# Squares of the first input held as whole tiles and summed by two engines in turn, and a pooling state stored in long rows

## The chip, the cores and the metric

The kernel runs on one core of one Trainium2 chip. The metric is the time of one execution on the device in microseconds (us), as the median over several runs. A core has five engines that run their own queues of instructions in order and wait for one another by semaphores: PE (TensorE, matmuls; PEld is its loading of weights), DVE (VectorE), ACT (ScalarE), POOL (GpSimd) and SP (SyncE, which here issues DMAs). DMAs are issued from the queues of SP, ACT and POOL; "SPq" and "ACTq" in a row mean the issuing instruction in that queue.

## The reference

One step of a decoder of two layers, for a prompt of 1024 positions and for 8 sample rows of one position each. All is float32; D is 1024.

```
layer 0: h = rmsnorm(x); z = h @ w_in_ab          # columns: pooling mixer | RWKV-7
         mix = concat(pool_mix(z[:512]), rwkv7_mix(z[512:])) @ w_out_ab
layer 1: h = rmsnorm(x); mix = sgu_mix(h)          # gated MLP with position mixing
each:    x += mix; x += cross_attn(rmsnorm(x)); x += relu(rmsnorm(x) @ w_up)**2 @ w_down
last:    y = rmsnorm(x)
rmsnorm(x) = x * rsqrt(mean(x*x) + eps) * g
pool_mix: new state of a sample row = its last 15 rows of (old state of 15 rows, new row)
```

The outputs are y, the keys and values of the memory tokens, and the new states, among them the pooling state of the 8 sample rows (8 x 15 x 512 numbers), which the kernel stores as a tensor `ps` of 128 partitions x 480.

## The kernel before

Activations lie transposed: a tile is 128 channels by 1032 columns (1024 prompt positions and the 8 sample rows), and eight such tiles make up x. Matmuls are exact to float32 by splitting each operand into a high and a low part and adding three products (high-high, high-low, low-high); `split` makes the parts, the high one on ACT (L194 without, L197 with a scale) and the low one on DVE (L195, L198). Columns are worked on in three groups GR of 384, 384 and 264. Large tiles come from 42 slots that `get` and `put` hand out first in, first out; `m2` hands out pieces of 512 columns from a ring of four buffers. The tile framework fills each engine's queue, as a rule in the order in which the code is written, sometimes with an instruction put ahead, and adds the waits.

The first place of the change is the very start. `xs` below is new; before, the loop at L544 loads a tile of x (L547), splits it (L197 on ACT, L198 on DVE), and calls `Stats.add` for each of the three column groups. `Stats.add` squares on ACT (L261 for the first tile, L264 for the others, into an `m2` buffer) and adds the square to the accumulator on GpSimd (L265). The matmuls of the loop (L565) need only the split parts: two blocks of output columns (units 16 and 17 of w_in_ab) are accumulated over all eight tiles in six PSUM banks, 18 matmuls for a tile. After the loop `finish` sums the accumulator over the partitions by small matmuls (L271), scales on DVE (L273) and takes the power -1/2 on GpSimd (L274), and `spread` writes it along the columns (L287 on PE, L289 on ACT) as the row by which every output is multiplied (L607 on DVE). Only then are the six PSUM banks emptied, so the next block's matmuls (`linear_g`, L225 to L227) wait for all of this. That block's weights were loaded and are cast on ACT (L194) when the buffer that block 16 used is free, and their low part is made on GpSimd (L195 in POOL's queue, since WZ[0] is 1), ahead of L274 in its queue.

The second place lies 375 us later, where the recurrent part has begun. Its chain of small matmuls (`Chain`, L1175 to L1217) goes on beside three other streams: the pooling mixer (`pooling`, L931), the inverses of small triangular blocks on DVE (`inverses`, L907 and L908, then ACT L911 and the stores L912 and L913 to `xid`), and the keys of the memory tokens (`memkv`, L1028 to L1033: a block of weights loaded by SP L204, split, 24 matmuls, scaled by L1032, stored by L1033). At the end of `pooling` SP stores the new states: L969 the prompt's, L970 the samples'. The samples' state lies in `pb4`, 32 runs of 16 numbers on each partition, of which L970 stores the last 15 of each run, in a DMA of 4096 pieces of 15 numbers. Behind it in SP's queue stand the last store of the pooling mixer (L967), a store of keys (L1033), the next load of weights (L204), and the stores of the inverses. ACT's queue issues the loads of the recurrent part (L1124 to L1137), among them L1131.

A DMA counts on one of eight semaphores, taken in turn over all DMAs of SP and ACT, and waits until the DMA eight before it has landed; these waits stand in the rows of the queues as waits for a semaphore.

Of the kernel before, what the change touches and what calls it, by code (L numbers as in the profile page):

```python
# [13 lines left out]
AF = mybir.ActivationFunctionType  # L14
ALU = mybir.AluOpType
# [9 lines left out]
GR = ((0, 384), (384, 768), (768, 1032))  # L25
# [100 lines left out]
def hybrid_step(ctx: ExitStack, tc: tile.TileContext, I, O):  # L126
    nc = tc.nc
    te, ve, se, po, sy = nc.tensor, nc.vector, nc.scalar, nc.gpsimd, nc.sync
# [5 lines left out]
    def nm(s="t"):  # L134
        uid[0] += 1
        return f"{s}{uid[0]}"
# [5 lines left out]
    def get(dt=F32):  # L142
        i = free.popleft()
        t = sb.tile([128, T], dt, tag=f"s{i}", name=nm("s"))
        owner[id(t)] = (i, t)
        return t

    def put(*ts):
        for t in ts:
            free.append(owner.pop(id(t))[0])  # L150

    def small(shape, tag, bufs=2, dt=F32):
        return sb.tile(shape, dt, tag=tag, bufs=bufs, name=nm(tag))
# [10 lines left out]
    def cyc(key, tags):  # L164
        turn[key] = turn.get(key, -1) + 1
        t = tags[turn[key] % len(tags)]
        return ps_of(t, 2 if t == "lin" else 1)
# [6 lines left out]
    def psm():  # L174
        return cyc("m", ("in0", "in1", "c0b", "c1b") if wide[0] else ("in0", "in1"))
# [11 lines left out]
    def pc(name, i):  # L187
        c = PCOL[name] + i
        return par[:, c : c + 1]


    def split(src, hi, lo, scale=None, eng=None):
        if scale is None:
            se.copy(out=hi, in_=src)  # L194
            (eng or ve).tensor_tensor(out=lo, in0=src, in1=f(hi), op=ALU.subtract)  # L195
        else:
            se.activation(out=hi, in_=src, func=AF.Copy, scale=scale)  # L197
            ve.scalar_tensor_tensor(out=lo, in0=src, scalar=scale, in1=f(hi), op0=ALU.mult, op1=ALU.subtract)  # L198
# [93 lines left out]
    def hpair():  # L292
        return get(F32R), get(F32R)
# [233 lines left out]
    st0 = Stats()  # L527
    first, fraw = [], []

    def fload(j, c0, c1_):  # L530
        if j == len(first):
            raw = sb.tile([128, 1024], F32, tag="wraw", bufs=2, name=nm("wr"))
            hi, lo = [sb.tile([128, 1024], F32R, tag=t, bufs=2, name=nm(t)) for t in ("whi", "wlo")]
            fraw.append(raw)
            first.append((16 + j, (hi, lo)))
        raw, (hi, lo) = fraw[j], first[j][1]
        sy.dma_start(out=raw[:, c0:c1_], in_=wab[16 + j][:, c0:c1_])
        split(raw[:, c0:c1_], hi[:, c0:c1_], lo[:, c0:c1_])
# [2 lines left out]
    sy.dma_start(out=par, in_=I["par"])  # L541
    psf = {}
    h = []
    for m in range(KT):  # L544
        x, hp = get(), hpair()
        for g0, g1 in GR if m == 0 else ((0, T),):
            sy.dma_start(out=x[:, g0:g1], in_=I["xT"][m][:, g0:g1])  # L547
            split(x[:, g0:g1], hp[0][:, g0:g1], hp[1][:, g0:g1], pc("mix0", m))
        for g0, g1 in GR:
            st0.add(m, g0, g1, x[:, g0:g1])  # L550
        h.append(hp)
        put(x)
        if m == 0:
            fload(1, 0, 256)
        if m == 1:
            fload(0, 256, 1024)
            fload(1, 256, 1024)
            sy.dma_start(out=ident, in_=I["ident"])
        ks = slice(m * 128, (m + 1) * 128)
        for j, (u, (wh, wl)) in enumerate(first):  # L560
            for g, (g0, g1) in enumerate(GR):
                if m == 0:
                    psf[u, g] = cyc("f", ("lin", "lin", "c0a", "c1a", "c0b", "c1b"))[:, : g1 - g0]
                for i, (w, a) in enumerate(((wh, hp[0]), (wh, hp[1]), (wl, hp[0]))):
                    te.matmul(psf[u, g], w[:, ks], a[:, g0:g1], start=m == 0 and i == 0, stop=m == KT - 1 and i == 2)  # L565
    for g in range(3):
        st0.finish(g)
    tick()
# [84 lines left out]
    def bulk(n=1):  # L653
        for _ in range(n):
            next(zs_, None)
            if side and next(side[0], 0) == 0:
                side.popleft()
# [268 lines left out]
    pb4 = pbuf[:, 0:512].rearrange("p (g b t) -> p g b t", g=4, b=8)  # L926
    pin = pbuf[:, 512:992]
# [3 lines left out]
    def pooling():  # L931
        for g in range(4):
            zused[0] = zorder.index(g)
            while g not in zready:
                bulk()
                yield
            zused[0] += 1
            z = zready.pop(g)
            win = WIN[g]
            po.tensor_copy(out=ppo[:, g, :], in_=z[:, NP - 15 : NP])  # L940
            po.tensor_copy(out=pb4[:, g, :, 15:16].rearrange("p b t -> p (b t)"), in_=z[:, NP:T])
            cur, step = z, 1
            while step < win:
                nx = get()
                eng = (po, ve)[PG[{1: 0, 2: 4, 4: 8, 8: 12}[step] + g]]
                eng.tensor_tensor(out=nx[:, step:NP], in0=cur[:, step:NP], in1=cur[:, 0 : NP - step], op=ALU.add)
                po.tensor_copy(out=nx[:, 0:step], in_=cur[:, 0:step])
                if cur is not z:
                    put(cur)
                cur, step = nx, step * 2  # L950
            d = get()
            o = C1["cnt"][0] + 16 * g
            ve.scalar_tensor_tensor(out=d[:, 16:NP], in0=cur[:, 16:NP], scalar=1.0 / win, in1=z[:, 16:NP], op0=ALU.mult, op1=ALU.subtract)
            ve.tensor_tensor(out=cur[:, 0:16], in0=cur[:, 0:16], in1=c1[:, o : o + 16], op=ALU.mult)
            ve.tensor_tensor(out=d[:, 0:16], in0=cur[:, 0:16], in1=z[:, 0:16], op=ALU.subtract)
            t = small([128, 8], "pws")
            ve.tensor_reduce(out=t, in_=pb4[:, g, :, 16 - win : 16], axis=AX.X, op=ALU.add)
            ve.scalar_tensor_tensor(out=d[:, NP:T], in0=t, scalar=1.0 / win, in1=z[:, NP:T], op0=ALU.mult, op1=ALU.subtract)
            put(cur)
            bulk()  # L960
            for _ in range(PLY):
                yield
            for g0, g1 in GR:
                ps = psm()
                te.matmul(ps[:, : g1 - g0], g2t[:, 512 + g * 128 : 640 + g * 128], d[:, g0:g1], start=True, stop=True)
                se.activation(out=z[:, g0:g1], in_=ps[:, : g1 - g0], func=AF.Copy, scale=pc("psc", g))
            sy.dma_start(out=mixd[g], in_=z)  # L967
            put(z, d)
        sy.dma_start(out=O["pp"], in_=ppo)  # L969
        sy.dma_start(out=O["ps"].rearrange("p (n t) -> p n t", t=15), in_=pb4[:, :, :, 1:16].rearrange("p g b t -> p (g b) t"))  # L970
        put(pbuf, g2t, c1)
        yield

# [289 lines left out]

    segs = [[(0, n)] * (n < 4) + [(1, n - 1)] * (n > 0) for n in range(5)]
    pg = pooling()

    def start(n):
# [897 lines left out]
```

## Time and profile before

| what | before |
|---|---|
| median of 3 runs | 3179.05 us |
| lowest and highest run | 3176.22 and 3179.43 us |
| the profiled execution's own time | 3185.59 us |
| its span, first to last instruction | 3183.8 us |
| mean granted TensorE clock | 0.983 |
| busy: PE, DVE, ACT, POOL | 97%, 66%, 43%, 23% of the span |

The profile is one execution seen by the hardware profiler. A row of a timeline begins with its start in us from the start of the span and its length in us, then the engine, the line of the code, the operation, and the tiles (buffer numbers left out); "x3" means three such instructions merged into one row, with the length from the first to the end of the last. Brackets at the end give the idle time of the engine before the row and what ended it. A row of the windows view gives the start and end of a stretch, and for each engine its busy time and number of instructions, then the TensorE clock that was granted (1.00 is full), the mean share of time in which the 16 DMA engines were busy (overlapping transfers count twice), and what they moved in GB/s. A row of the grouped lines ends in its total, the mean in ns of one, and the idle time before.

### The profile page before, as it was taken

The numbers are of one execution on the slowest core, as the hardware profiler recorded it, in microseconds if no ns is written. First come the engines' busy times: TensorE is split into PE (matmuls) and PEld (weight loads), VectorE is DVE, ScalarE is ACT, GpSimd is POOL, SyncE is SP. The second block draws the span as 40 slices with busy tenths as digits, with TensorE's granted clock in tenths as the row PEclk, the third lists the DMA queues.
The fourth block names the chain that finished last, engine by engine and source line by source line (L and its number), as shares of the span: only waits on it lengthen the run. The fifth ranks groups of instructions, "written<-read, shape, count | busy, mean of one in ns | idle before, by whom it ended". The sixth has DMA issues, their size and how long they took to land. (4 is left out here: it accounts for less than half of the span.)

```text
span 3183.8 us, 59345 instructions
## 1 busy us (share of the span) xinstructions
PE 3081.0 (97%) x23514; PEld 2957.1 (93%) x23514; DVE 2086.6 (66%) x3778; ACT 1353.3 (43%) x2757; POOL 717.3 (23%) x650
## 2 busy tenths in 40 slices
PE   8999889999999999999999999999999999999998
PEld 7987778899899999999999999899989999999998
DVE  4688734644457887566787776656455788765775
ACT  5223234433345444544455454614334544453443
POOL 5233424320021223022131100223001122211213
PEclk9999989999999999999999999999999999999999
DMA  3346577643522444866522223524343244476643
GB/s 119 117 132 208 88 247 234 209 140 120 180 87 103 158 160 173 218 174 174 174 89 99 88 94 138 204 80 143 113 147 120 94 158 156 164 236 140 181 166 121
DMA packets 215846, 473.25 MB, mean 149 GB/s; under 512 B 47374, under 2 KB 72334, under 8 KB 215567
## 3 DMA queue, kind: packets, MB, share of 16 engines
q1 hardware_dynamic: 188814, 423.63, 39.0%
q0 software_dynamic: 6912, 25.37, 4.6%
q10 hardware_dynamic: 19840, 20.45, 2.3%
q8 instruction: 185, 3.03, 0.4%
q14 instruction: 95, 0.77, 0.1%
HBM read 309.87 MB, written 159.50 MB: 147 GB/s over the span
## 5 line engine op out<-in xcount | busy, mean ns | idle before, releaser
L454 PE MATMUL ps<-s,wp 128*128 128x258 f32 x3584 | 1018.7, 284 | 11.3 <-DVE s L490 5.9
L456 PE MATMUL ps<-s,wp 128*128 128x258 f32 x3584 | 1013.2, 283 | 4.4 <-DVE wp L195 4.2
L455 PE MATMUL ps<-s,wp 128*128 128x258 f32 x3584 | 1014.1, 283 | 0.0
L454 PEld LDWEIGHTS ps<-s,wp 128*128 128x128 f32 x3584 | 677.8, 189 | 15.2 <-DVE s L490 6.7
L456 PEld LDWEIGHTS ps<-s,wp 128*128 128x128 f32 x3584 | 678.9, 190 | 5.7 <-DVE wp L195 5.7
L455 PEld LDWEIGHTS ps<-s,wp 128*128 128x128 f32 x3584 | 680.5, 190 | 0.2 <-issue 0.2
L225 PE MATMUL ps<-s,wh 128*128 128x384 f32 (+2 forms) x1994 | 649.5, 327 | 19.3 <-ACT wh L194 16.5
L226 PE MATMUL ps<-s,wh 128*128 128x384 f32 (+2 forms) x1994 | 643.6, 323 | 0.1
L227 PE MATMUL ps<-s,wl 128*128 128x384 f32 (+2 forms) x1994 | 640.0, 322 | 0.4 <-DVE wl L195 0.4
L225 PEld LDWEIGHTS ps<-s,wh 128*128 128x128 f32 x1994 | 380.6, 191 | 30.4 <-ACT wh L194 17.3
L226 PEld LDWEIGHTS ps<-s,wh 128*128 128x128 f32 x1994 | 381.1, 191 | 7.9 <-issue 6.0
L227 PEld LDWEIGHTS ps<-s,wl 128*128 128x128 f32 x1994 | 380.0, 191 | 6.0 <-issue 4.1
L265 POOL TENSOR_TENSOR s<-s,m 128x384 f32<-128x384 f32 (+1 forms) x147 | 162.0, 1110 | 652.6 <-ACT m L264 651.7
L194 ACT CAST s<-s 128x516 fp32r<-128x516 f32 (+6 forms) x316 | 199.2, 657 | 144.2 <-DMA s<-hts 32.5
L195 DVE TENSOR_TENSOR wp<-wr,wp 128x512 fp32r<-128x512 f32 x200 | 159.9, 800 | 89.9 <-ACT wp L194 88.1
L194 ACT CAST wh<-wr 128x1024 fp32r<-128x1024 f32 x110 | 115.1, 1047 | 200.1 <-PE ps L226 155.1
L194 ACT CAST wp<-wr 128x512 fp32r<-128x512 f32 x200 | 124.5, 622 | 129.1 <-issue 48.3
L195 DVE TENSOR_TENSOR wl<-wr,wh 128x1024 fp32r<-128x1024 f32 x97 | 121.5, 1254 | 58.5 <-ACT wh L194 53.9
L195 DVE TENSOR_TENSOR s<-s,s 128x516 fp32r<-128x516 f32 (+6 forms) x148 | 122.5, 841 | 52.2 <-ACT s L194 40.5
L225 PE MATMUL ps<-s,s 128*128 128x384 f32 (+3 forms) x432 | 142.9, 333 | 6.9 <-ACT s L1768 6.5
L195 DVE TENSOR_TENSOR s<-s 128x516 fp32r<-128x516 f32 x168 | 116.3, 726 | 37.5 <-ACT s L194 37.0
L226 PE MATMUL ps<-s,s 128*128 128x384 f32 (+3 forms) x432 | 139.6, 323 | 0.0
(346 smaller groups left out, 5271.3 us busy)
## 6 DMA issues: line engine op xcount, KB each, us to landing
hdn<-s SPq DMA_DIRECT2D x128, 258.0 KB, 2.1
hts<-s SPq DMA_DIRECT2D x48, 516.0 KB, 2.7
s<-hts SPq DMA_DIRECT2D x96, 258.0 KB, 6.6
xf<-s POOLq DMA_DIRECT2D x48, 516.0 KB, 7.5
s<-hdn SPq DMA_DIRECT2D x72, 258.0 KB, 5.4
s<-in_wd SPq DMA_DIRECT2D x34, 512.0 KB, 5.2
s<-in_kc SPq DMA_DIRECT2D x64, 256.0 KB, 3.6
s<-in_vc SPq DMA_DIRECT2D x64, 256.0 KB, 3.1
```

The source lines that it names most:

```text
L194: se.copy(out=hi, in_=src)
L195: (eng or ve).tensor_tensor(out=lo, in0=src, in1=f(hi), op=ALU.subtract)
L225: te.matmul(out, wh, xh, start=i == 0, stop=False)
L226: te.matmul(out, wh, xl, start=False, stop=False)
L227: te.matmul(out, wl, xh, start=False, stop=i == n - 1)
L265: po.tensor_tensor(out=self.acc[:, g0:g1], in0=self.acc[:, g0:g1], in1=sq, op=ALU.add)
L454: te.matmul(out, wh, xh, start=j < 4 and k == 0, stop=False, skip_group_check=j >= 4)
L455: te.matmul(out, wh, xl, start=False, stop=False, skip_group_check=j >= 4)
L456: te.matmul(out, wl, xh, start=False, stop=k == 3, skip_group_check=j >= 4)
```

## The change

At the first place the squares are no longer taken group by group. A tile's square is taken by one ACT instruction over all 1032 columns into a slot of its own (the first tile's straight into the accumulator), and it is added by one instruction: on GpSimd for odd tiles, on DVE for even ones. This is done when two more tiles of x have been split; the last two squares follow after the loop. At the second place GpSimd first copies the 32 x 15 numbers of each partition into `pin` (the loaded old state, no longer needed), and the DMA stores `pin`, 480 numbers in a row on each partition.

```
+    def squares(m, x):
+        if m == 0:
+            se.activation(out=st0.acc, in_=x, func=AF.Square)
+        else:
+            sq = get()
+            se.activation(out=sq, in_=x, func=AF.Square)
+            (po if m % 2 else ve).tensor_tensor(out=st0.acc, in0=st0.acc, in1=sq, op=ALU.add)
+            put(sq)
+        put(x)
+    xs = deque()
     for m in range(KT):
...
-        for g0, g1 in GR:
-            st0.add(m, g0, g1, x[:, g0:g1])
+        xs.append((m, x))
         h.append(hp)
-        put(x)
+        if len(xs) > 2:
+            squares(*xs.popleft())
...
+    while xs:
+        squares(*xs.popleft())
     for g in range(3):
         st0.finish(g)
...
-        sy.dma_start(out=O["ps"].rearrange("p (n t) -> p n t", t=15), in_=pb4[:, :, :, 1:16].rearrange("p g b t -> p (g b) t"))
+        po.tensor_copy(out=pin.rearrange("p (n t) -> p n t", t=15), in_=pb4[:, :, :, 1:16].rearrange("p g b t -> p (g b) t"))
+        sy.dma_start(out=O["ps"], in_=pin)
```

How the queues change. First DVE's queue at the start, from the low part of the third tile to the first scaling in `finish`; `s_69` is the accumulator, each other `s` a slot, and par the table of scales. Before:

```order
L198 SCALAR_TENSOR_TENSOR s_166<-s_164,par,s_165 128x1032
L198 SCALAR_TENSOR_TENSOR s_199<-s_197,par,s_198 128x1032
L198 SCALAR_TENSOR_TENSOR s_232<-s_230,par,s_231 128x1032
L198 SCALAR_TENSOR_TENSOR s_265<-s_263,par,s_264 128x1032
L198 SCALAR_TENSOR_TENSOR s_298<-s_296,par,s_297 128x1032
L198 SCALAR_TENSOR_TENSOR s_331<-s_329,par,s_330 128x1032
L273 TENSOR_SCALAR rst_366<-ps_362 128x3
```

And now:

```order
L198 SCALAR_TENSOR_TENSOR s_154<-s_152,par,s_153 128x1032
L552 TENSOR_TENSOR s_69<-s_69,s_210 128x1032
L198 SCALAR_TENSOR_TENSOR s_179<-s_177,par,s_178 128x1032
L198 SCALAR_TENSOR_TENSOR s_206<-s_204,par,s_205 128x1032
L198 SCALAR_TENSOR_TENSOR s_233<-s_231,par,s_232 128x1032
L552 TENSOR_TENSOR s_69<-s_69,s_264 128x1032
L198 SCALAR_TENSOR_TENSOR s_260<-s_258,par,s_259 128x1032
L198 SCALAR_TENSOR_TENSOR s_287<-s_285,par,s_286 128x1032
L552 TENSOR_TENSOR s_69<-s_69,s_312 128x1032
L273 TENSOR_SCALAR rst_322<-ps_318 128x3
```

Three additions now stand between the low parts: that of tile 2 ahead of tile 3's low part, that of tile 4 ahead of tile 6's, and that of tile 6 after the last.

GpSimd's queue at the same place had 21 additions of one column group each (14 of 128x384, 7 of 128x264) ahead of the low part of the next weights (L195) and the powers. Now:

```order
L552 TENSOR_TENSOR s_69<-s_69,s_183 128x1032
L552 TENSOR_TENSOR s_69<-s_69,s_237 128x1032
L552 TENSOR_TENSOR s_69<-s_69,s_291 128x1032
L552 TENSOR_TENSOR s_69<-s_69,s_315 128x1032
L195 TENSOR_TENSOR wl_463<-wr_461,wh_462 128x1024
L274 TENSOR_TENSOR rs_71<-rst_322,mhalf 128x3
```

The 21 have become four whole ones, for tiles 1, 3, 5 and 7; what follows them stands in the same order as before.

At the second place, GpSimd's queue from the last column group of the pooling mixer. The row of 128x1023 is the first doubling step of the window sums and the COPY rows of 1, 2, 4 and 8 columns fill the first columns of each step. Before:

```order
L941 COPY s_2948<-s_3333 128x8
L946 TENSOR_TENSOR s_3582<-s_3333 128x1023
L947 COPY s_3585<-s_3582 128x2
L1120 MEMSET s_2967 64x1024
L947 COPY s_3588<-s_3585 128x4
```

And now:

```order
L956 COPY s_2904<-s_3289 128x8
L961 TENSOR_TENSOR s_3538<-s_3289 128x1023
L985 COPY s_2904<-s_2904 128x480
L962 COPY s_3541<-s_3538 128x2
L1136 MEMSET s_2923 64x1024
L962 COPY s_3544<-s_3541 128x4
```

The new copy of 480 columns stands behind the first doubling step and ahead of the copy of two columns. SP's queue keeps its order there (the state's store, then L967, L1033, L204, L912, L913 by the old numbers); only the store itself goes from 4096 pieces to 128 rows. On all engines the rest of the program stands in the same order as before, save a few matmuls of the first loop and the statistics that changed places with neighbours.

## The prediction

> **What bounds the kernel now.** I read the page first, then the windows of the two places that the change touches, then their timelines engine by engine.
>
> ```profile
> PE 3081.0 (97%) x23514; PEld 2957.1 (93%) x23514; DVE 2086.6 (66%) x3778; ACT 1353.3 (43%) x2757; POOL 717.3 (23%) x650
> ```
>
> PE is busy nearly all of the span, so only what PE waits for, or a slower clock, can be won. The change removes no matmul. At the start, in stretches of 10 us:
>
> ```profile
> 30.00:40.00 10.00, 8.09 (x53) 7.65 (x53) 1.61 (x3) 4.82 (x7) 10.00 (x9) 0.98 0.00 0
> 40.00:50.00 10.00, 9.03 (x43) 9.03 (x44) 6.58 (x12) 2.11 (x4) 3.64 (x8) 0.67 0.33 106
> ```
>
> Here GpSimd (the fifth pair) is busy all 10 us and PE is not. The timelines of GpSimd and of the others show how it sets the pace:
>
> ```profile
> 10.86 26.94 POOL L265 TENSOR_TENSOR s<-s,m 128x384 f32<-128x384 f32 x21 [10.02 <-ACT m L264]
> 37.76 2.34 POOL L195 TENSOR_TENSOR wl<-wr,wh 128x1024 fp32r<-128x1024 f32 x1
> 40.06 2.90 POOL L274 TENSOR_TENSOR rs<-rst,mhalf 128x3 f32<-128x3 f32 x3
> ```
>
> ```profile
> 18.83 0.69 PE L565 MATMUL ps<-s,whi 128*128 128x384 f32 x3
> 21.65 0.33 PE L565 MATMUL ps<-s,whi 128*128 128x384 f32 x1
> ...
> 30.78 0.43 ACT L264 ACTIVATE m<-s 128x264 f32<-128x264 f32 x1 [1.40 <-POOL s L265]
> 31.11 1.15 ACT L197 ACTIVATE s<-s,par 128x1032 fp32r<-128x1032 f32 x1
> 33.64 0.44 PE L565 MATMUL ps<-s,whi 128*128 128x384 f32 x1 [0.58 <-DVE s L198]
> 35.07 1.05 ACT L194 CAST wh<-wr 128x1024 fp32r<-128x1024 f32 x1 [0.16 <-PE ps L565]
> 36.41 2.27 PE L271 MATMUL ps<-ones,s 128*128 128x1 f32 x18
> 40.97 4.01 PE L287 MATMUL ps<-ident,rs 128*128 128x128 f32 x18 [2.29 <-POOL rs L274]
> 44.84 0.67 PE L225 MATMUL ps<-s,wh 128*128 128x384 f32 x1
> ```
>
> The 21 additions run without a gap, 26.94 us. ACT squares into a ring of four buffers, so it waits for GpSimd (1.40 us ahead of L264), tile 7's L197 comes late behind that, and PE waits for the low part (0.58). Tile 3 took PE 21.65 - 18.83 = 2.82 us without a wait; the last tile ends where L271 starts, at 36.41. When the additions end (37.8), the weights' low part (2.34) goes ahead of the powers, which start at 40.06, and the next block at 44.84. So the additions bound this stage twice.
>
> At the second place the rows are those of SP's queue, the landing times of three of its DMAs (the state, the keys, the weights, in this order), the wait inside the load's issue, and one window:
>
> ```profile
> 375.48 0.57 SPq L970 DMA_DIRECT2D out_ps<-s  x1
> 377.11 6.14 SPq L967 DMA_DIRECT2D mixd<-s  x1
> 383.34 0.56 SPq L1033 DMA_DIRECT2D out_mk<-m  x1
> 398.00 0.33 SPq L204 DMA_DIRECT2D wr<-in_wk  x1
> ...
> 401.95 5.26 SPq L204 DMA_DIRECT2D wr<-in_wk  x2
> ```
>
> ```profile
> DMA to landing us min/median/max: 17.9/17.9/17.9
> ```
>
> ```profile
> DMA to landing us min/median/max: 3.4/7.9/14.6
> ```
>
> ```profile
> L204 SPq EVENT_SEMAPHORE  x4: 17/22/14024, 383.9 to 414.0; - x4
> ...
> DMA to landing us min/median/max: 5.5/7.3/9.9
> ```
>
> ```profile
> 380.00:385.00 5.00, 0.70 (x16) 0.56 (x12) 5.00 (x8) 0.37 (x1) 3.80 (x4) 0.60 2.06 23
> ```
>
> The store L970 needs 17.9 us for 240 KB; around it the DMA engines are full (share 2.06) and move 23 GB/s. The issue behind it, L967, takes 6.14 us. The keys' store L1033, issued at 383.34, is the one of 14.6 us: it lands at 397.9. The load of the next weights waits 14.02 us, from 383.9, for exactly that, and is issued at 398.00. PE feels it:
>
> ```profile
> 394.44 0.28 PE L227 MATMUL ps<-s,wl 128*128 128x256 f32 x1
> 405.65 0.58 PE L225 MATMUL ps<-s,wh 128*128 128x256 f32 x1 [10.93 <-ACT wh L194]
> ```
>
> ```profile
> 385.77 1.22 DVE L195 TENSOR_TENSOR wl<-wr,wh 128x1024 fp32r<-128x1024 f32 x1
> ...
> 392.17 0.42 DVE L1032 TENSOR_TENSOR m<-ps,s 128x256 f32<-128x256 f32 x1 [1.24 <-PE ps L227]
> ...
> 411.99 0.42 DVE L1032 TENSOR_TENSOR m<-ps,s 128x256 f32<-128x256 f32 x1 [4.80 <-PE ps L227]
> ```
>
> ```profile
> 398.53 0.58 ACT L966 ACTIVATE s<-ps,par 128x384 f32<-128x384 f32 x1 [17.43 <-DMA s<-xid]
> ...
> 404.55 1.04 ACT L194 CAST wh<-wr 128x1024 fp32r<-128x1024 f32 x1 [3.15 <-DMA wr<-in_wk]
> ...
> 410.61 1.05 ACT L194 CAST wh<-wr 128x1024 fp32r<-128x1024 f32 x1 [0.25 <-DMA wr<-in_wk]
> ```
>
> PE stands still for 10.93 us for weights that were issued late. ACT, too, stood 17.43 us ahead of L966, its queue held by DMA issues that wait for the same slow DMAs.
>
> **The change part by part.** *Squares.* What a whole tile costs must come from other rows:
>
> ```profile
> 16.71 2.04 DVE L198 SCALAR_TENSOR_TENSOR s<-s,par,s 128x1032 fp32r<-128x1032 f32 x1
> 21.18 1.29 DVE L198 SCALAR_TENSOR_TENSOR s<-s,par,s 128x1032 fp32r<-128x1032 f32 x1 [2.42 <-ACT s L197]
> 81.70 1.22 DVE L755 TENSOR_TENSOR s<-s,s 128x1032 f32<-128x1032 f32 x1
> ```
>
> ```profile
> L946 POOL TENSOR_TENSOR s<-s 128x1023 f32<-128x1023 f32 x2 | 4.7, 2374 | 0.0
> L929 POOL COPY s<-s 128x480 f32<-128x480 f32 x1 | 0.6, 583 | 1.4 <-DMA s<-in_sp 1.4
> ```
>
> A whole addition is 1.22 us on DVE (L755) and 2.37 on GpSimd (L946); ACT's whole square is about as long as its L197, 1.15, against three of about 0.43 (L264 at 30.78), and has a slot of its own, so ACT's waits for the ring go. ACT then needs some 2.3 us a tile, DVE 1.29 and half an addition, GpSimd 1.2 on average: each under PE's 2.82, so PE paces the loop. From tile 4 (21.65) it needs 4 x 2.82 and ends at 32.9, 3.5 us earlier. The sum is one chain, though, each addition behind the one before, on two engines. DVE's L198 took 2.04 us beside busy additions (at 16.71) and 1.29 in a gap, so I let the two engines exclude each other. From 16.71, when tile 2's L198 is done: addition 2 to 17.9, L198 of tile 3 to 19.2, addition 3 (GpSimd) to 21.6, tiles 4 and 5 to 24.2, addition 4 to 25.4, tile 6 to 26.7, addition 5 to 29.1, tile 7 to 30.4, addition 6 to 31.6, addition 7 to 34.0. Tile 4's low part comes 0.3 late for PE, the others in time: PE ends at 33.2. The weights' cast follows PE as before (35.07 against 36.41), now 31.9 to 32.9, so GpSimd starts the weights' low part when the chain ends, 34.0, and the powers at 34.0 + 2.34 = 36.3 instead of 40.06: **3.8 us** won. All that follows hangs on these powers and moves with them. Bounds: with no exclusion the chain ends ahead of the cast (32.6) and the powers start at 34.9, 5.2 won; with every GpSimd addition twice as long and DVE's at 2.04, the chain from 11.5 is 4 x 4.75 + 3 x 2.04 = 25.1, ends at 36.6, and 1.1 is won. I take 3.8, since the row at 16.71 is of this very pair. [...]
>
> *The store.* The copy costs GpSimd about 0.58 us (L929 is the same shape the other way round). It stands ahead of the copy of two columns that DVE needs:
>
> ```profile
> 378.03 0.18 POOL L947 COPY s<-s 128x2 f32<-128x2 f32 x1
> ...
> 379.86 1.21 DVE L946 TENSOR_TENSOR s<-s 128x1022 f32<-128x1022 f32 x1
> ```
>
> That copy ended at 378.21 and DVE came to it at 379.86, so 1.65 us are free and 0.58 is hidden. SP now waits at the store until 378.6, 3 us longer; behind it L967 (ready at 377.1) goes at 379, L1033 at 379.4 instead of 383.34, both earlier, since the 6.14 us of issue go with the small pieces. The keys then land well before 387, and the load of weights is held only by its buffer, which DVE's L195 frees at 385.77 + 1.22 = 387.0. With the lag of before (398.00 to 404.55, 6.55) the cast starts at 393.5 and is done at 394.6, when PE ends the work in hand: the gap of 10.93 closes. What is late next is the load after it. It stands behind the keys' store of 392.17 + 0.42, so it is issued at 393.0 instead of 401.95. With the lag of before (401.95 to 410.61, 8.66, in which ACT's queue also waited for the reloads of xid) its cast is at 401.7 and PE goes on at 402.8; PE was at that point at 412.0 (411.99, the end of the block): 9.2 won. With the shortest landing, 5.5, PE goes on at 399.7 and 12.3 are won. Against it stands the clock: PE's new gap of 2 to 5 us may leave it slower for a while, as the clock of 0.60 in the window at 380 shows after the stop there; a block of about 2.8 us at half the clock costs 2.8 more. [...] I take the middle, 10.75, less 1 for the clock: **9.7 us**, bounds 6.4 (9.2 less 2.8) and 12.3. Later loads and reloads are behind PE's progress or one another and move along.
>
> *Slots.* The squares take seven more slots in turn, at a point where fewer than 42 have been handed out, so none waits; the later rotation shifts, and the order of work stays. I price that at nothing; a wait that it opened would be one landing, 5 to 8 us.
>
> The sum is 3.8 + 9.7 = 13.5 us. The profiled execution took 3185.59 us, 6.5 above the median 3179.05, so it would come to 3172.1; the same gain on the median gives **3165.5**.
>
> **The rivals.** (1) The gap fills up again: ACT's queue, or the reloads of xid behind DMA engines that are full anyway at 400, take over as PE's last wait. For it: ACT stood still 17.43 us for DMAs. Against: the waits on record end with the DMAs queued behind L970. Then 3.8 and some 1.5 of the store remain: 3173.7. (2) The sum chain becomes the bound: doubled additions leave 1.1 of the first term, 1.1 + 9.7: 3168.2. For it the row of 2.04, against it the gaps that four additions leave on GpSimd. (3) Slower: the new copy. It holds GpSimd ahead of the two-column copy; beyond 1.65 us each us of it delays DVE's L946 and, in DVE's queue, the inverses and both weights' low parts, one for one. It decides from 1.65 + 13.5 = 15.2 us on; at 20 us the time would be 4.8 more than before, 3183.9. For it: GpSimd's spans are rough and a strided copy is seen only once. Against: that once was 0.58.
>
> **How the numbers follow.** The forecast has 75%, rival 1 12%, rival 2 10%, rival 3 3%. The forecast's own bounds are 3.8 - 2.7 + 6.4 = 7.5 and 5.2 + 12.3 = 17.5 won, 3171.6 to 3161.6; with the runs' own spread (some 3 us) and rival 1 the range is 3157 to 3175. A measurement of this kernel can tell 0.2%, 6.4 us, from no change. Rival 1 lies within that; the forecast and rival 2 are beyond it, but for the runs' spread. Faster 0.84, same 0.13, slower 0.03.
>
> **What would show it.** Right: ACT's idle times for L265 gone; four additions of 2.4 to 3.7 us; the powers near 36; the state's store landing within about 3 us; the load of weights issued near 387 less the first gain; no 10.93 us ahead of L225. Wrong: a gap of the same size ahead of that L225 with another releaser, low parts that PE waits for in the loop, or a second place that is quicker while the end of the recurrent part stays put.

## The result, and the profile after

The changed kernel takes 3158.79 us (median of 4 runs, 3156.12 to 3165.26) against 3179.24 for the kernel before (4 runs, 3176.22 to 3182.09): ratio 0.9934, 95% interval 0.9918 to 0.9951, or 20.4 us less. A second measurement of the same pair, further below, gave 0.9948 (0.9934 to 0.9962), 16.5 us less. The forecast was 3165.5, 13.5 less: right in direction and place, and 3 to 7 us short. The forecast's own bounds on the gain ended at 17.5 us; the first measurement lies beyond them, and within the range only by the allowance for the runs' spread. The profiled execution took 3157.35 us, 1.4 below its median.

The page's first lines, of the kernel after: the span, then busy time and count for each engine.

```profile
span 3155.6 us, 59305 instructions
...
PE 3067.4 (97%) x23514; PEld 2945.7 (93%) x23514; DVE 2094.8 (66%) x3781; ACT 1351.0 (43%) x2741; POOL 701.0 (22%) x634
```

PE has the same 23514 matmuls. GpSimd and ACT lost 16 instructions each and DVE gained three. No engine's total explains 20 us; the two places do.

**The start.** GpSimd's timeline of the kernel after (start, duration; in brackets the idle time before, and what ended it):

```profile
11.63 2.59 POOL L552 TENSOR_TENSOR s<-s,s 128x1032 f32<-128x1032 f32 x1 [10.78 <-ACT s L551]
18.40 3.38 POOL L552 TENSOR_TENSOR s<-s,s 128x1032 f32<-128x1032 f32 x1 [4.18 <-DVE s L552]
25.36 3.34 POOL L552 TENSOR_TENSOR s<-s,s 128x1032 f32<-128x1032 f32 x1 [3.59 <-DVE s L552]
31.09 2.41 POOL L552 TENSOR_TENSOR s<-s,s 128x1032 f32<-128x1032 f32 x1 [2.38 <-DVE s L552]
33.99 2.35 POOL L195 TENSOR_TENSOR wl<-wr,wh 128x1024 fp32r<-128x1024 f32 x1 [0.49 <-ACT wh L194]
36.31 2.90 POOL L274 TENSOR_TENSOR rs<-rst,mhalf 128x3 f32<-128x3 f32 x3
```

GpSimd now waits between its additions, and ACT no longer waits for it. The additions end at 33.50, and what GpSimd waits for after that (0.49 us) is ACT's cast. The powers start at 36.31, against 40.06 before. DVE in the same stretch:

```profile
18.17 5.90 DVE L198 SCALAR_TENSOR_TENSOR s<-s,par,s 128x1032 fp32r<-128x1032 f32 x3
24.00 1.22 DVE L552 TENSOR_TENSOR s<-s,s 128x1032 f32<-128x1032 f32 x1
```

The first row merges three L198. The one in the middle, taken alone:

```profile
19.38 3.50 DVE L198 SCALAR_TENSOR_TENSOR s<-s,par,s 128x1032 fp32r<-128x1032 f32 x1
```

It started while GpSimd's addition ran (18.40 to 21.78) and ended 1.1 us after it; the two others took 1.28 each. The addition, too, was longer (3.38) than the last one (2.41): it had started while the first L198 ran. DVE's own addition took 1.22. PE's waits for low parts in the loop are three, 2.8 us in total, where the kernel before has six, 4.4 us. PE and ACT show how the stage ends:

```profile
22.93 0.44 PE L578 MATMUL ps<-s,whi 128*128 128x384 f32 x1 [0.60 <-DVE s L198]
...
34.21 2.07 PE L271 MATMUL ps<-ones,s 128*128 128x1 f32 x18
...
41.08 0.67 PE L225 MATMUL ps<-s,wh 128*128 128x384 f32 x1
```

```profile
32.87 1.05 ACT L194 CAST wh<-wr 128x1024 fp32r<-128x1024 f32 x1 [7.83 <-PE ps L578]
```

PE's last tile ends at 34.21 (before 36.41), the cast at 33.92, and the next block starts at 41.08 instead of 44.84: 3.76 us won.

**The second place**, which now comes about 7 us earlier. SP's queue of the kernel after, and its store's time to landing:

```profile
371.76 0.34 SPq L986 DMA_DIRECT2D out_ps<-s  x1
372.19 0.38 SPq L982 DMA_DIRECT2D mixd<-s  x1
372.67 0.45 SPq L1049 DMA_DIRECT2D out_mk<-m  x1
380.16 0.34 SPq L204 DMA_DIRECT2D wr<-in_wk  x1
```

```profile
DMA to landing us min/median/max: 4.9/4.9/4.9
```

The store lands after 4.9 us instead of 17.9, the issue behind it takes 0.38 instead of 6.14, and the keys' store goes out 0.9 us after the state's (before, 7.9). The load of weights leaves 7.5 us behind the keys' store instead of 14.7. The new copy on GpSimd and the step of DVE behind it:

```profile
371.07 0.67 POOL L985 COPY s<-s 128x480 f32<-128x480 f32 x1
371.68 0.36 POOL L962 COPY s<-s 128x2 f32<-128x2 f32 x1
```

```profile
373.01 1.21 DVE L961 TENSOR_TENSOR s<-s 128x1022 f32<-128x1022 f32 x1
```

The copy took 0.67 us, the two columns were there at 372.04, and DVE came to them at 373.01 without a wait. On PE the gap of 10.93 us has shrunk to this, and the windows show DMA engines that move data all through:

```profile
393.41 0.38 PE L225 MATMUL ps<-s,wh 128*128 128x256 f32 x1 [1.66 <-ACT wh L194]
```

```profile
375.00:380.00 5.00, 1.72 (x3) 1.14 (x4) 5.00 (x13) 0.00 (x0) 3.71 (x5) 0.50 0.78 231
380.00:385.00 5.00, 5.00 (x23) 4.39 (x23) 3.73 (x9) 3.10 (x3) 1.39 (x2) 0.55 0.95 356
385.00:390.00 5.00, 5.00 (x43) 4.93 (x42) 2.08 (x3) 1.05 (x1) 0.27 (x1) 1.00 1.04 379
390.00:395.00 5.00, 3.34 (x52) 2.80 (x51) 1.76 (x3) 2.69 (x4) 0.00 (x0) 0.97 0.83 271
395.00:400.00 5.00, 5.00 (x35) 4.88 (x34) 1.21 (x2) 0.61 (x2) 0.00 (x0) 0.69 0.85 237
```

The last two columns are DMA share and GB/s: 231 to 379 GB/s, where the kernel before moved 23 in its window from 380 to 385.

### The profile page after: what moved, and what is told of

It is laid out like the page before. It is cut to its first block, busy times and chain, and to the rows that moved or that the text cites. A ratio compares the mean times of both kernels' runs of the same rounds, so it can differ in the third digit from the quotient of the medians.

```text
span 3155.6 us, 59305 instructions
## 1 busy us (share of the span) xinstructions
PE 3067.4 (97%) x23514; PEld 2945.7 (93%) x23514; DVE 2094.8 (66%) x3781; ACT 1351.0 (43%) x2741; POOL 701.0 (22%) x634
## 5 line engine op out<-in xcount | busy, mean ns | idle before, releaser
L265 POOL TENSOR_TENSOR s<-s,m 128x384 f32<-128x384 f32 (+1 forms) x126 | 135.6, 1079 | 644.8 <-ACT m L264 643.8
L195 DVE TENSOR_TENSOR wp<-wr,wp 128x512 fp32r<-128x512 f32 x200 | 160.5, 803 | 83.0 <-ACT wp L194 82.0
L195 DVE TENSOR_TENSOR s<-s,s 128x516 fp32r<-128x516 f32 (+6 forms) x148 | 122.7, 842 | 55.1 <-ACT s L194 54.1
L195 DVE TENSOR_TENSOR wl<-wr,wh 128x1024 fp32r<-128x1024 f32 x97 | 121.9, 1258 | 53.6 <-ACT wh L194 48.7
L195 DVE TENSOR_TENSOR s<-s 128x516 fp32r<-128x516 f32 x168 | 116.6, 730 | 38.1 <-ACT s L194 37.6
```

Source lines behind the costliest of these rows:

```text
L265: po.tensor_tensor(out=self.acc[:, g0:g1], in0=self.acc[:, g0:g1], in1=sq, op=ALU.add)
```

## The experiments

Two theories stood at first. **Mine:** the squares give 3.8 us, the store some 10, and the store's part comes from the 4096 pieces that fill the DMA engines. **The rival:** one half carries nearly all, or the surplus over 13.5 us comes from elsewhere (the copy, the slots, the order). In microseconds a ratio is taken of about 3180.

**Each half alone, and both kernels again.** e1 is the kernel after with the old store:

```diff
-        po.tensor_copy(out=pin.rearrange("p (n t) -> p n t", t=15), in_=pb4[:, :, :, 1:16].rearrange("p g b t -> p (g b) t"))
-        sy.dma_start(out=O["ps"], in_=pin)
+        sy.dma_start(out=O["ps"].rearrange("p (n t) -> p n t", t=15), in_=pb4[:, :, :, 1:16].rearrange("p g b t -> p (g b) t"))
```

e2 is the kernel before with the new copy and store (the same edit the other way round); e3 and e4 are the two kernels unchanged.

> The squares as whole tiles, the state's store as before. My theory (two separate gains): the powers after the loop start near 36.3 us instead of 40.06, and the whole kernel gains that 3.8 us, 1 to 5, so some 3175; the 10.9 us of PE ahead of the second weights of the memory keys stay, and the state's store still takes 16 to 18 us to land. Rival (the early start is what lets the second place go faster, by meeting the DMA queues at another moment): 10 us or more are gained here too, and the gap ahead of that load is mostly gone.

> The squares as before, the state copied on GpSimd and stored in long rows. My theory: 10 to 17 us are gained, so 3162 to 3169, the powers stay at 40.06, the load of weights behind the store is issued within a us of 387, the gap of 10.9 us is gone. With the squares' own gain the two parts make up the change's 20.4. Rival (half of the 20.4 lies in neither place but in a later shift): both parts alone stay below 8 us.

> The kernel before once more, unchanged. It gives the spread of one program between executions and a second profile. All theories expect a ratio of 1 within 0.2%. My theory expects the gap of 10 to 11 us and a landing of 16 to 18 us in this profile as well; if the drift of offsets between 41 and 375 us that I see between the first two profiles (3 us) is the spread of executions, this profile shows drifts of like size against the first one.

> The changed kernel once more, unchanged: 3159, 3155 to 3165, and a second profile in which the powers start at 36.3 and no wait of PE between 380 and 395 is over 6 us. If the 7 us by which the profiles differ more than the medians are spread of executions, this profile's span lies some 3 to 8 us above the first one's 3155.6.

| kernel | ratio to before (95%) | us won |
|---|---|---|
| e1, squares alone | 0.9991 (0.9979 to 1.0003) | 2.9 (-1 to 6.7) |
| e2, store alone | 0.9956 (0.9942 to 0.9971) | 14.0 (9 to 18) |
| e3, before again | 1.0003 (0.9992 to 1.0013) | -1 (-4 to 2.5) |
| e4, after again | 0.9948 (0.9934 to 0.9962) | 16.5 (12 to 21) |

The parts add up within these intervals, 2.9 + 14.0 = 16.9 against 16.5, so nothing shows that one needs the other. e1's time is not told from no change; its place is: its powers start at 36.10, and PE's wait at the second place is all there still. PE's waits for the weights there (total, times, longest), in e1 and then in e2:

```profile
PE ps L225 <- ACT wh L194: 15.6, 2, 14.1
```

```profile
PE ps L225 <- ACT wh L194: 2.1, 1, 2.1
```

e2 has the old start (its powers start at 40.38, 0.3 us behind those of before), so its times can be laid beside those of the prediction directly. Its SP queue, and PE at the one wait that is left:

```profile
378.83 0.34 SPq L971 DMA_DIRECT2D out_ps<-s  x1
...
387.23 0.34 SPq L204 DMA_DIRECT2D wr<-in_wk  x1
...
392.03 2.70 SPq L204 DMA_DIRECT2D wr<-in_wk  x2
```

```profile
398.86 1.04 ACT L194 CAST wh<-wr 128x1024 fp32r<-128x1024 f32 x1 [1.32 <-DMA wr<-in_wk]
```

```profile
399.96 0.38 PE L225 MATMUL ps<-s,wh 128*128 128x256 f32 x1 [2.13 <-ACT wh L194]
...
412.10 0.65 PE L1183 MATMUL ps<-s,s 128*64 128x64 f32 x8 [0.79 <-DMA s<-vd]
```

Store at 378.83 (forecast 378.6), load at 387.23 (387.0), the next one at 392.03 (393.0): the queue went as worked out. The cast came 6.83 us behind that last issue, not 8.66, and PE went on at 399.96, not 402.8: 12.0 us won at that point. Further on the kernel before loses more; these are waits of its PE that the prediction did not price:

```profile
422.05 0.39 PE L225 MATMUL ps<-s,wh 128*128 128x256 f32 x1 [1.48 <-ACT wh L194]
...
425.81 1.08 PE L1182 MATMUL ps<-s,s 128*64 128x64 f32 x8 [1.99 <-POOL gnq L1231]
```

In e2 only the 0.79 above stands at these two points, so 2.68 us more are won. DVE's multiplications L1032, which follow PE's blocks one by one, are 11.0 us earlier in e2 at 417.46 and 420.30 of before, and 15.0 at 430.61 and 436.13. Of this rise of 4.0, the two waits are 2.7. The other 1.3 is PE's clock, in the stretch between the two pairs, first in before and then in e2:

```profile
420.30:430.61 10.31, 6.84 (x104) 6.14 (x104) 2.42 (x4) 4.91 (x9) 2.69 (x2) 0.83 0.79 259
```

```profile
409.32:415.58 6.26, 5.47 (x104) 4.88 (x106) 2.33 (x5) 2.87 (x6) 2.70 (x2) 1.00 1.03 336
```

The same 104 matmuls kept PE busy for 6.84 us at a mean granted clock of 0.83 and for 5.47 us at 1.00: 1.4 us.

**No store, and pieces put back.** If the DMA engines' time is the cause, the rows and the copy should cost nothing measurable, and an extra store of 4096 pieces into a scratch tensor, with the rest of the change in place, should take the store's gain away. e6 drops the copy and the store; e5 is the kernel after with this line behind L986:

```diff
+        sy.dma_start(out=scr.rearrange("p (n t) -> p n t", t=15), in_=pb4[:, :, :, 1:16].rearrange("p g b t -> p (g b) t"))
```

> The changed kernel with the old store of 4096 pieces added again beside the new one, into a scratch tensor that nothing reads. My theory (the pieces fill the DMA queues, and the DMAs queued behind them are late): the loss of before comes back although the state is also stored in rows; the extra store lands after 16 to 18 us, PE stands 8 to 14 us ahead of the second weights behind it, and the time is 11 to 18 us over the changed kernel's. Rival (the gain came from GpSimd's copy moving the other work, or from the instruction's new place): it stays within 4 us of the changed kernel.

> The changed kernel without the copy and without the store of the samples' pooling state (that output is not written). It gives what the row store and the copy still cost. My theory: next to nothing, within 2 us of the changed kernel, since 0.67 us of copy lies in slack and the store lands in 5 us with nothing waiting on it. Rival (the row store still delays the load behind it): 3 us or more are gained and the remaining wait of 1.7 to 3.0 us ahead of the weights is gone.

e6: 0.9943 (0.9922 to 0.9963), the same as the kernel after, so what is left of the store costs nothing that shows. e5: 0.9995 (0.9982 to 1.0007), and the gain is gone, to within the 4 us that such an interval leaves. Nothing holds the extra store back for the copy, so in SP's queue it stands ahead of the state's store (369.88 against 373.02), near the place of the old store in e1 (368.8). In e5 the extra store's landing and PE's waits for weights read:

```profile
DMA to landing us min/median/max: 17.4/17.4/17.4
```

```profile
PE ps L225 <- ACT wh L194: 12.4, 3, 7.1
```

The loss comes back in three waits, the longest 7.1 us, and not in one of 8 to 14 us as I had expected.

**Half the pieces, another queue, another time.** This was to tell three readings of the pieces' harm apart: the time of the DMA engines, the queue that issues them, or the place. e10 has the extra store with 2048 pieces, e11 with 4096 from GpSimd's queue, and e9 is the kernel before with its old store moved some 210 us later (held there by one pass of ACT over 512 columns of the state, scaled by a one, `late`, worked out from a late result); in this order:

```diff
+        sy.dma_start(out=scr.rearrange("p (n t) -> p n t", t=15)[:, 16:32], in_=pb4[:, 2:4, :, 1:16].rearrange("p g b t -> p (g b) t"))
```

```diff
+        po.dma_start(out=scr.rearrange("p (n t) -> p n t", t=15), in_=pb4[:, :, :, 1:16].rearrange("p g b t -> p (g b) t"))
```

```diff
-        sy.dma_start(out=O["ps"].rearrange("p (n t) -> p n t", t=15), in_=pb4[:, :, :, 1:16].rearrange("p g b t -> p (g b) t"))
...
+    se.activation(out=pbuf[:, 0:512], in_=pbuf[:, 0:512], func=AF.Copy, scale=late[:, 0:1])
+    sy.dma_start(out=O["ps"].rearrange("p (n t) -> p n t", t=15), in_=pb4[:, :, :, 1:16].rearrange("p g b t -> p (g b) t"))
```

> The changed kernel with an extra store of half the pieces (the last two groups, 2048 pieces) into a scratch tensor at the old place. My theory: landing time goes with the number of pieces, 8 to 10 us; the load behind it is then held to about 379 to 381 of its own time, where its buffer comes free anyway, so that most of the loss stays away: 0 to 6 us over the changed kernel, against 13 for the whole. Rival (the loss is in proportion to the pieces): 6 to 9 us over the changed kernel.

> The changed kernel with the extra store of 4096 pieces issued from GpSimd's queue instead of SP's. It asks whether SP's and ACT's own queues were full or the DMA engines themselves. If the engines are what is full (my theory): the loads of SP and ACT are late as before, most of the 13 us are lost. If only the queue is (rival): the landing is as long, SP and ACT go on, and the time stays within 4 us of the changed kernel, unless GpSimd's issue holds up its copies of the pooling steps (an issue row of over 2 us would show that).

> The kernel before, with the store of 4096 pieces as it was but 220 us later, when the recurrent part ends (one ACT pass over its buffer, scaled by a one that is made from the last recurrent state, ties it there). My theory (the pieces cost by what is queued behind them): the 14 us of the second place come back as in the kernel with the store alone, near 387 to 412; at the new place the loads of the first input stand behind the store, so part is lost again, 0 to 10 us, and the time lies between 3165 and 3177. Rival (pieces cost the time that they take wherever they stand): 12 us or more are lost at the new place, the time stays at that of before.

e10: 0.9979 (0.9969 to 0.9990), 6.7 us won, so some 10 of the 16.5 are lost by the times. By the traces, the DVE steps that before has at 430 come 15.0 us earlier in e10, 21.4 in the kernel after and 6.0 in e5: half the pieces lose 6.4, all lose 15.4. I had expected that half the pieces would do little harm, with the load of weights leaving at 379 to 381; it left at 382.85. The loss grows with the pieces; whether still fewer would be free is not shown. Landing of e10's 2048 pieces, and PE's waits for weights:

```profile
DMA to landing us min/median/max: 9.4/9.4/9.4
```

```profile
PE ps L225 <- ACT wh L194: 5.9, 3, 4.8
```

e11: 0.9992 (0.9979 to 1.0005), the gain is gone as in e5. Its store's issue on GpSimd, landing, SP's load of weights, and who waited:

```profile
L988 POOL DMA_DIRECT2D scr<-s x1: 1857/1857/1857, 373.1 to 373.1; - x1
...
DMA to landing us min/median/max: 21.9/21.9/21.9
```

```profile
382.88 0.34 SPq L204 DMA_DIRECT2D wr<-in_wk  x1
```

```profile
ACT wh L194 <- DMA wr<-in_wk: 22.3, 3, 15.3
...
PE ps L225 <- ACT wh L194: 14.7, 2, 14.0
```

SP's queue is free here: state's store, L983 and keys' store go out within 1 us (372.89 to 373.80), and the load leaves at 382.88. It is the load itself that lands late, and ACT waits up to 15.3 us for it. The queue is therefore not the cause; what the queues share is, the DMA engines or something behind them, which these runs do not tell apart. In the kernel before the same shortage showed as a late issue, because the keys' store, which took 14.6 us to land, was caught in it.

e9: 0.9966 (0.9954 to 0.9979), 10.8 us won, so moving the pieces regains most of the 14.0. At their new place they fill the DMA engines just as much; its windows there:

```profile
590.00:595.00 5.00, 5.00 (x32) 5.00 (x32) 4.90 (x10) 2.31 (x4) 0.00 (x0) 1.00 2.03 67
595.00:600.00 5.00, 5.00 (x31) 5.00 (x30) 4.70 (x9) 3.46 (x6) 0.00 (x0) 1.00 1.27 12
```

Share 2.03 and down to 12 GB/s, as at 380 in the kernel before, and yet PE is busy all the time: here nothing that PE needs soon is in a load. One wait of 3.4 us for weights follows. In these runs, what 4096 pieces cost is what is queued behind them: 14.0 us at the old place, 3.2 at the new one (14.0 less 10.8).

**The exclusion, and the additions all on DVE.** The prediction rested its 3.8 us on the two engines excluding each other. e7 takes GpSimd out; e8 takes also the first weights' low part to DVE (first entry of WZ):

```diff
-            (po if m % 2 else ve).tensor_tensor(out=st0.acc, in0=st0.acc, in1=sq, op=ALU.add)
+            ve.tensor_tensor(out=st0.acc, in0=st0.acc, in1=sq, op=ALU.add)
-WZ = (1, 0, 0, 1, 0, 0, 1, 0, 1, 0, 0, 0, 1, 0, 0, 1)
+WZ = (0, 0, 0, 1, 0, 0, 1, 0, 1, 0, 0, 0, 1, 0, 0, 1)
```

> The changed kernel with all seven additions of squares on DVE. My theory (GpSimd and DVE shut each other out): the low parts L198, 1.94 us on average where a GpSimd addition ran (5.90 us for three, 4.66 for two), all take 1.28 to 1.30, PE's waits for them go, and the powers start 0.8 to 1.5 us earlier than 36.3, bound by the cast of the next weights. Rival (something else stretches them, the loads of x that land at the same time): the low parts stay at 1.9 us and over, and DVE with 2.5 us a tile becomes late, the powers start at 37 us or later.

> As the one with all additions on DVE, and the low part of the first block of weights after the loop on DVE as well, so that GpSimd has only the powers. My theory: the powers start when the statistics are there, near 34.0 us, 2.3 earlier than in the changed kernel, and the kernel gains 2 to 3 us on it, which the times can hardly tell (0.1%). Rival (the low part on DVE delays the scaling of the statistics and the first outputs): the powers start at 35 or later, nothing is gained.

e7's DVE and GpSimd:

```profile
19.04 3.70 DVE L198 SCALAR_TENSOR_TENSOR s<-s,par,s 128x1032 fp32r<-128x1032 f32 x3
```

```profile
31.66 2.35 POOL L195 TENSOR_TENSOR wl<-wr,wh 128x1024 fp32r<-128x1024 f32 x1 [30.81 <-ACT wh L194]
33.97 2.90 POOL L274 TENSOR_TENSOR rs<-rst,mhalf 128x3 f32<-128x3 f32 x3
```

The three L198 take 3.70 us, none over 1.29, where they took 5.90 beside GpSimd's addition, while the DMA engines, the other suspect, were as busy there as before (share 1.02 to 1.07 from 16 to 24 us, against 1.03 to 1.07): it is GpSimd's addition that stretched them. DVE does seven additions instead of three, PE's waits for L198 sink from 2.8 to 0.9 us, and the powers start at 33.97, 2.3 us earlier than after the change (I had expected 0.8 to 1.5). In e8 the powers start at 33.59 and the block behind them at 37.42 (41.08 after the change). e8's time, 0.9947 (0.9930 to 0.9963), is not told from that of the kernel after, and e7, one run, took 3166.36. So the forecast's assumption held in these traces, the alternation leaves some 2 us at the start that all-DVE additions would not, and whether these 2 us reach the end stays open.

## Why the prediction was right, and where it was short

**The squares** came out as worked out: 3.8 forecast, 3.76 at the next block. Two steps on the way differed and cancelled, so that the agreement to within 0.1 us is luck. PE waited for late L198s, the last time 0.60 us in the row above, and ended at 34.21 instead of 33.2; the chain ended at 33.50 instead of 34.0. So the cast behind PE, not the chain, released the low part, at 33.99 where 34.0 was forecast. The 33.2 does not follow from the prediction's own chain: that has tile 4's low part done at 22.9 (24.2 less the 1.29 of tile 5), and the row at 21.65 has PE ready for it at 21.98, so it is 0.9 late and not 0.3, and PE ends near 33.8. The sign that PE waits for low parts in the loop did show; it put the cast 0.4 us behind the end of the chain.

One reading behind the exclusion was wrong: the L198s of 1.29 us did not run "in a gap", since GpSimd added without one. It was GpSimd's addition that stretched. Beside the L198 at 21.18 stands this one, where one of its shape that started with no L198 under way took 1.0 us (24.03):

```profile
21.29 2.05 POOL L265 TENSOR_TENSOR s<-s,m 128x384 f32<-128x384 f32 x1
```

The exclusion holds all the more: in these rows the one that starts second is the one that stretches. This addition, started 0.11 us behind an L198, took 2.05 us; the L198 at 16.71, started during GpSimd's addition of 15.66 to 17.67, took 2.04; and after the change it is 3.50 us for the L198 that started during GpSimd's addition, against none over 1.29 in e7.

Nor did all that follows just move with the powers. The L1032 of before at 378.78 came 6.9 us earlier in the kernel after and 5.6 to 7.9 earlier in six other profiles with the same start (e1, e4, e5, e6, e10, e11), while the second profile of before (e3) differs by 0.1. The mean granted clock from 45 to 370 us was 0.97 in before and 0.99 in after; that this is the cause is not shown, and e1's time does not show the 3 us at the end.

**The store** was mis-sized: 9.7 forecast, 14.0 by the times. Up to the issue of the second load each time of the queue was right within 1 us, though the store took 4.6 us (4.9 in the kernel after) to land and not 3. Two steps of the sum failed. The first is the middle value of 10.75 between the lag of before, 8.66, and the shortest landing, 5.5: the lag was 6.83 and the gain 12.0, near the other end (12.3). The second is the sentence that later loads "move along": two more waits of PE in before, 1.48 and 1.99 us, were late results of the same jam and went too, to 0.79, and with them 1.4 us of a slowed clock. The charge of 1 us for the clock agrees with e2, whose gain sank from 12.0 to 11.0 us by 417 of before, with its clock at 0.50 behind the new stop (below). The half clock that this charge counted on stands in the trace of before as well, 0.50 in every window of 1 us from 382 to 390; how long a stop must be to bring it, no run shows.

**The slots** and **the copy** cost nothing that shows, as forecast: ACT's squares L551 have no idle time ahead of them, and e6 without the copy is no faster. No run tests the later rotation of the slots by itself.

**The rivals.** That the gap fills again (1) had a true part, waits of 1.66 and 2.13 us for the next load, but not its size. That the sum chain becomes the bound (2) came near: it ended 0.4 us ahead of the cast. The slower case (3) needed a copy of over 15.2 us; it took 0.67.

**What stays open:** the 3 us by which the second place came earlier than the start explains, and the difference between 16.5 and 20.4 us of the two measurements, whose intervals overlap. The two profiled executions of the kernel after differ by 5 us in span (3155.6 and 3160.7), and at equal instructions two profiles of the kernel before differ by up to 3.4 us, so offsets late in the program say no more.

## What to carry to other kernels

A store of many small pieces was priced here by what stood behind it in every queue until it landed (17.9 us for 4096 pieces, 14.0 us of the kernel's time): turn it into rows with a copy on an engine that has time (0.67 us on GpSimd), or move it to a place where nothing needed soon is loaded (10.8 of the 14.0 came back). When such a jam goes, follow the loads on to the next two or three waits, since late work further down is part of its price (2.68 us in two waits here). When work is shared between DVE and GpSimd, count the DVE instructions that stretch beside it (L198 from 1.28 to 3.50 us); GpSimd, with 2.41 us for an addition that took DVE 1.22, may cost more than it takes over (with all seven on DVE the powers started 2.3 us earlier).

## What the runs showed of the hardware

- 4096 pieces of 60 bytes took 17.4 to 19.9 us to land from SP's queue, 21.9 from GpSimd's; 2048 took 9.4; the same 240 KB in 128 rows took 4.5 to 4.9. In these runs the time goes with the number of pieces, 4.2 to 5.3 ns each.
- An issue from GpSimd's queue of 4096 pieces held GpSimd for 1.86 us (L988 of e11); from SP the same issue took 0.53 to 0.57.
- A short stop of PE was followed by a slower clock in three profiles; in a fourth it was not. In the kernel after, PE stood still for 1.66 us ahead of 393.41, with narrow matmuls around (28 of 128x32 ahead of the stop), and from 395 on the granted clock was 0.50, in windows of 1 us:

```profile
394.00:395.00 1.00, 1.00 (x11) 0.85 (x8) 0.72 (x2) 0.97 (x2) 0.00 (x0) 0.86 0.44 123
395.00:396.00 1.00, 1.00 (x9) 0.88 (x8) 1.00 (x1) 0.61 (x2) 0.00 (x0) 0.50 0.59 161
...
398.00:399.00 1.00, 1.00 (x9) 1.00 (x9) 0.00 (x0) 0.00 (x0) 0.00 (x0) 0.94 0.98 361
```

  e2 and e4 show the same behind their stops of 2.13 and 3.02 us (0.50 at 403 to 405 and at 396 to 398). e6 does not: at the same place it stood for 2.72 us, and its clock was 1.00 in every window up to 400:

```profile
393.14 0.38 PE L225 MATMUL ps<-s,wh 128*128 128x256 f32 x1 [2.72 <-ACT wh L194]
```

  In the kernel after, too, the clock stayed at 1.00 behind a stop of 2.65 us ahead of 1296.61. So the length of a stop does not decide alone, and what does is not shown here. In the kernel after, a gap that had been closed from 10.93 us down to 1.66 was still followed by some 3.4 us at half the clock (by the windows of 1 us: 0.3 us of the one from 394, all of 395 to 398, 0.1 of the one from 398).
